# Another clock for the planner that orders a hybrid decoder block: memory told apart by space, durations as measured, eight transfers at once

## The chip, the cores and the metric

The kernel runs on one core of a Trainium2 chip. Its time is the device time of one execution in microseconds (us), here the median of three runs; less is better. The engines named below are PE (TensorE, matrix products, with PEld for its weight loads), DVE (VectorE), ACT (ScalarE), POOL (GpSimd) and SP (SyncE, which issues every DMA). Each engine works through its own instructions strictly in the order in which they were written, so one that waits holds up all that stand behind it on its engine.

## The reference

One decoder block over 2048 tokens of width 1024, all in fp32. An input x is RMS-normed and modulated, and one projection w_in makes 9344 columns of it; two causal token mixers work on them, and three more products bring the result back to the residual stream.

```python
h = _rmsnorm(x, norm_g) * (1.0 + scale) + shift
p = einsum('bsd,de->bse', h, w_in)
c_val, c_gate, c_og, ts, r_og, g_conv, g_rwkv = split(p)
# conv branch: u = val*sigmoid(gate); 31-tap causal depthwise conv; LayerNorm; silu; * silu(c_og); @ w_conv_out
# rwkv branch, per head (16 heads of 64), for every token t:
sk = state @ kk_t
state = state * w_t - sk b_t^T + v_t k_t^T
out_t = state @ r_t
# then a norm over each head, + bonus, * silu(r_og), @ w_rwkv_out
# merge by sigmoid gates g_conv, g_rwkv; @ w_out; residual; final RMSNorm
```

## The kernel before, in words

**Tiling.** Tokens are taken in 4 blocks of 512. w_in has 73 tiles of 128 columns; one projection is 8 slices of the inner dimension by 3 matmuls, since each fp32 operand is split into a high and a low half (h_hi, h_lo; w_hi, w_lo) and high·high, high·low and low·high are summed: 24 "big" matmuls of 128x512 into a PSUM bank called ps_main. In block 0 a weight arrives as w_st, ACT casts its high half w_hi, POOL or DVE subtracts for w_lo, and both halves are stored (kh_in, kl_in) and only loaded again in blocks 1 to 3.

**What runs between the projections.** Per channel tile, the 31 taps of the convolution run on DVE with the sum in PSUM (acc<-u,ck,acc). The recurrence works in chunks of 64 tokens on groups of 4 heads: 16 groups (4 per block, each of two pairs). A group forms masked matrices As, stores a part of them (dA), loads it in another layout (La, with norms dn), inverts triangles on POOL in 31 steps (itmp, TT), stores the result (dT), loads it back into As (As<-dT), transposes on DVE (Tn, Qs) and makes a few products (late, aux, xo are the small PSUM banks; tk, uv and KR are operands of the chain). Then comes its serial chain: 8 steps, each xo<-S,KR on PE, an addition into uv on DVE, xo<-uv,tk on PE, and four updates of the state S on DVE. A group norm follows (gst, POOL, ACT, DVE, grs, POOL: uv<-uv,grs), then two sets of four transposes late<-ident,uv, whose results go as oc through two POOL operations (with zb and zr) to the DRAM tile z_d.

**The output products.** Three products (ro, co, o) for each half of the tokens follow a scheme of seven block products; their weights (w_raw, split into the two halves of w_c) and their operands (cells, h_hi, h_lo) are loaded and split as they are needed. The first product uses two PSUM banks. The others use eight, and wait for that until the last group is normed (`wide[0] = 8` in `lend_cells`, set once the second set of transposes of the last group has been issued).

**What sets the order.** The Python code runs once, when the program is built, and plans with a clock of its own. Every instruction goes through a thin wrapper (`Lane`, so nearly every row of the profile has its line, L186, `r = f(*a, **k)`), which calls `note`. `note` estimates when the instruction starts and ends: `now` is the time of PE, `vt` the time at which each other engine and the DMA become free, `ready` and `used` when a tile is written and read. All side work is a `Task`, a generator that yields a condition: `ok(t)` (t is ready), `idle(engine, us)` (that engine is nearly free), `burst` and `joining` (ready, and some us more), `bank` and `room`. After each big matmul, `poll` lets those tasks go on whose time has come by that clock, and their instructions, small matmuls too, are put there. `until` moves the clock on where PE has nothing to do. `quick` and `some` choose DVE or POOL for a subtraction by which is free earlier, and `Load.steps` chooses so for w_lo. So a wrong estimate does not make a wrong result; it puts an instruction earlier or later in its engine's queue. Waits on the chip are by semaphores.

The estimates before: memory was told apart by the class of a tensor. All tiles from pools have one class, so PSUM tiles and DRAM tiles were both seen as SBUF, and only the kernel's own arguments as DRAM. A transfer takes bytes / 330e3 us on the one DMA time line, and lands 2.8 us later (1.9 if it writes the output). Inputs that are the same object as the output were left out, such as acc in the taps, and the wait between engines was 0.1 us.

Of the kernel before, what the change touches and what calls it, by code (L numbers as in the profile page):

```python
# [15 lines left out]
PSUM = bass.MemoryType.PSUM  # L16
DRAM = bass.MemoryType.DRAM
# [4 lines left out]
TB = 512  # L22
NTT = TB // P
CH = 64
# [38 lines left out]

XN = ((0, 1), (2, 3), (), ())
# [15 lines left out]
def hybrid_block(ctx: ExitStack, tc: tile.TileContext, x, vecs, convk, w2a2, final_g, ada, w_in, w_co, w_ro, w_o, crow, out,  # L80
# [24 lines left out]
    def note(name, op, out, ins, extra=0.0):  # L105
        k_ = key(out)
        t = max([now[0], vt.get(name, 0.0), used.get(k_, 0.0) if name != "PE" or k_[:2] != "xo" else 0.0] + [ready.get(key(a), 0.0) + SEM for a in ins])
        if k_ not in ready and getattr(out.tensor, "tag", None) and out.tensor.name not in cells_:
            past, n = tags.setdefault(out.tensor.tag, []), out.tensor.tag_meta.bufs
            free_ = sorted((max(ready.get(q, 0.0), used.get(q, 0.0)) for q in past), reverse=True)  # L110
            if len(free_) >= n:
                t = max(t, free_[n - 1])
            past.append(k_)
            del past[:-3 * n]
        if name == "PE":
            if op == "transpose":
                part, c = False, 0.11
            else:
                K_, M_, N_ = ins[0].shape[0], size(ins[0]), size(ins[1])
                part = K_ <= 64 or M_ <= 64  # L120
                c = max(N_, 64) / 600 * (0.27 if M_ <= 64 and K_ <= 64 else 0.53 if part else 1.04)
                if ins[1].dtype == F32R:
                    part, c = False, 0.015 + N_ / 2400
            if part != kind[0]:
                kind[0], c = part, c + (0.13 if part else 0.27)
            now[0] = t + c
            end = now[0] + 0.2
        elif name == "SP":
            vt["SP"] = t + 0.47 + (0.2 if k_[:2] in ("dT", "La", "dn") else 0.0)
            vt["DMA"] = max(vt["DMA"], t) + size(out) * out.shape[0] * 4 / DMA_RATE  # L130
            end = vt["DMA"] + (LOAD if on_chip(out) else 2.9 if k_[:2] == "dA" else STORE)
        else:
            n_ = max([size(out)] + [size(a) for a in ins[:1]])
            cols = sum(size(a) == 1 for a in ins[1:])
            wide = [a for a in ins if size(a) > 1]
            if name == "ACT":
                c = (0.065 if in_psum(ins[0]) else 0.105) + 0.82e-3 * n_ + 0.095 * cols + extra
                done_ = 0.1
            elif name == "DVE":
                c, done_ = 0.1 + 1.0e-3 * n_ + 0.05 * min(cols, 1), 0.08  # L140
                if op == "memset":
                    c = 0.1 + 0.9e-3 * n_
                elif n_ <= 16:
                    c = 0.18
                elif op == "scalar_tensor_tensor" and n_ == CH:
                    c = 0.31
                elif op == "tensor_tensor_scan":
                    c += 1.15e-3 * n_
                elif op == "transpose":
                    c += 0.2e-3 * n_  # L150
                elif op == "reciprocal":
                    c = 0.27
                elif in_psum(out):
                    c += 0.13
                elif len(wide) == 1 and not in_psum(ins[0]) and op in ("tensor_scalar", "tensor_copy"):
                    c -= 0.28e-3 * n_
                c += extra
            else:
                c, done_ = (0.1 + 0.72e-3 * n_ if op == "memset" else max(0.2, 0.1 + 2.25e-3 * n_)), 0.045
            both_ = name == "POOL" and op == "tensor_tensor" or name == "DVE" and sum(  # L160
                not in_psum(a) for a in wide) > 1
# [12 lines left out]
        for a in ins:  # L174
            used[key(a)] = max(used.get(key(a), 0.0), end)

    class Lane:
# [4 lines left out]
        def __getattr__(self, op):  # L182
            f = getattr(self.eng, op)

            def call(*a, **k):
                r = f(*a, **k)  # L186
                aps = [x_ for x_ in (*a, *k.values()) if hasattr(x_, "tensor") and hasattr(x_, "shape")]
# [240 lines left out]
    wide = [0]  # L428
# [1238 lines left out]
    with tc.manual_schedule():  # L1667
# [332 lines left out]
        out_ = [e1.tile([P, TB], F32, name=f"mr0_{n}", tag=t_) for n, t_ in  # L2000
                enumerate(("M", "ta", "E2", "k", "r", "vv", "y", "sh", "lw", "la", "E1", "sq"))]
# [210 lines left out]
```

## Time and profile before

| | |
|---|---|
| median of 3 runs | 2774.97 us (2773.39 to 2779.99) |
| profiled execution, its own time | 2775.74 us |
| its span | 2774.0 us |
| PE busy | 2627.9 us (95%) |
| DVE busy | 2225.7 us (80%) |
| POOL busy | 1275.3 us (46%) |
| ACT busy | 1185.1 us (43%) |
| DMA | 705.05 MB, mean 254 GB/s |

The profile is one execution. In a row of groups or of the timeline, "out<-in" are the tiles written and read (numbers left out), "x4" counts instructions, and the bracket gives the idle time of the engine before them and what ended it. A row of waits says which engine waited with which instruction for what, in total, how often and the longest. Matmuls overlap, so the busy time of a row of PE is longer than its share of the time: the mean of one big matmul is 404 ns in the groups, while PE starts one about every 0.23 us.

### The profile page before, as it was taken

To read this page: it belongs to the slowest core of one execution; us is meant where nothing else is said; L and a number is where in the kernel's file an instruction comes from. 1 tells how busy PE (TensorE), PEld (TensorE's weight loads), DVE (VectorE), ACT (ScalarE), POOL (GpSimd) and SP (SyncE) were. 2 spreads that over 40 slices of the span, in tenths; PEclk is the share of its full clock that TensorE was granted. 3 is DMA by queue.
4 is the path that set the end of the run, shared out by engine and by line. 5 is a ranking of instruction groups with operands and counts; after the bars stand their busy time and mean duration, and the time that the engine had idled before them with its cause. 6 is when DMAs were issued, how large, how long until landed. Compare 5 with 4: busy or idle time off the path is not lost. (4 is left out here: it accounts for less than half of the span.)

```text
span 2774.0 us, 51080 instructions
## 1 busy us (share of the span) xinstructions
PE 2627.9 (95%) x18416; PEld 2105.4 (76%) x18416; DVE 2225.7 (80%) x3824; ACT 1185.1 (43%) x2342; POOL 1275.3 (46%) x1791
## 2 busy tenths in 40 slices
PE   6989999999999999999999999999999988999997
PEld 5767777777777777778787878777777776788786
DVE  7777678897878787978788879889887578998586
ACT  5544445453334343434434434323434254546443
POOL 1464756551436654545574737366636557000000
PEclk9999999999999999999999999999999999999999
DMA  8776777866778868877776878777666767889874
GB/s 335 282 258 222 266 265 259 298 220 195 218 231 265 255 217 269 273 262 253 229 255 222 271 249 277 230 269 239 219 227 224 243 223 251 306 305 338 316 256 177
DMA packets 397167, 705.05 MB, mean 254 GB/s; under 512 B 138097, under 2 KB 154801, under 8 KB 396913
## 3 DMA queue, kind: packets, MB, share of 16 engines
q1 hardware_dynamic: 396912, 701.78, 75.2%
q8 instruction: 145, 2.38, 0.3%
q14 instruction: 110, 0.89, 0.1%
HBM read 487.26 MB, written 213.26 MB: 253 GB/s over the span
## 5 line engine op out<-in xcount | busy, mean ns | idle before, releaser
L186 PE MATMUL ps_main<-h_hi,w_lo 128*128 128x512 f32 x2304 | 931.5, 404 | 22.8 <-POOL w_lo L186 17.3
L186 PE MATMUL ps_main<-h_hi,w_hi 128*128 128x512 f32 x2304 | 930.9, 404 | 17.4 <-DMA w_hi<-kh_in 6.9
L186 PE MATMUL ps_main<-h_lo,w_hi 128*128 128x512 f32 x2304 | 927.2, 402 | 0.1
L186 DVE SCALAR_TENSOR_TENSOR acc<-u,ck,acc 128x512 f32<-128x512 f32 x928 | 698.4, 753 | 27.9 <-POOL u L186 0.2
L186 PEld LDWEIGHTS ps_main<-h_hi,w_lo 128*128 128x128 f32 x2304 | 437.8, 190 | 127.0 <-POOL w_lo L186 21.4
L186 PEld LDWEIGHTS ps_main<-h_hi,w_hi 128*128 128x128 f32 x2304 | 438.1, 190 | 118.1 <-issue 15.3
L186 PEld LDWEIGHTS ps_main<-h_lo,w_hi 128*128 128x128 f32 x2304 | 438.2, 190 | 95.3 <-issue 5.3
L186 PE MATMUL ps_main<-h_hi,w_c 128*128 128x512 f32 x896 | 293.7, 406 | 9.4 <-DVE w_c L186 3.2
L186 ACT ACTIVATE th<-ps_main 128x512 f32<-128x512 f32 x160 | 95.7, 598 | 325.2 <-PE ps_main L186 299.4
L186 POOL TENSOR_TENSOR itmp<-La,TT 128x126 f32<-128x126 f32 (+22 forms) x496 | 204.5, 412 | 47.0 <-issue 20.9
L186 POOL TENSOR_TENSOR TT<-TT,itmp 128x126 f32<-128x126 f32 (+22 forms) x496 | 205.3, 414 | 38.9
L186 POOL TENSOR_TENSOR w_lo<-w_st,w_hi 128x1024 fp32r<-128x1024 f32 x56 | 137.9, 2463 | 177.3 <-ACT w_hi L186 160.5
L186 PEld LDWEIGHTS ps_main<-h_hi,w_c 128*128 128x128 f32 x896 | 171.8, 193 | 51.7 <-DVE w_c L186 4.1
L186 DVE SCALAR_TENSOR_TENSOR S<-xo,pe,Se 64x64 f32<-64x64 f32 x512 | 144.9, 283 | 75.8 <-PE xo L186 55.6
L186 PE MATMUL ps_main<-h_lo,w_c 128*128 128x512 f32 x448 | 181.3, 405 | 6.1 <-DVE h_lo L186 5.1
L186 ACT COPY uv<-xo 64x256 f32<-64x256 f32 (+1 forms) x192 | 81.0, 438 | 238.6 <-PE xo L186 173.6
L186 PE MATMUL ps_main<-w_c,h_hi 128*128 128x512 f32 x448 | 140.3, 394 | 0.1
L186 DVE TENSOR_TENSOR As<-aux,maskA 128x512 f32<-128x512 f32 x128 | 82.3, 685 | 55.7 <-PE aux L186 55.0
L186 ACT CAST w_c<-w_raw 128x512 fp32r<-128x512 f32 x168 | 100.6, 617 | 56.1 <-DMA w_raw<-w_co_t 21.4
L186 ACT ACTIVATE t<-ps_main,mu 128x512 f32<-128x512 f32 x96 | 65.8, 685 | 128.6 <-PE ps_main L186 113.5
L186 ACT ACTIVATE Se<-S,pe 128x128 f32<-128x128 f32 x256 | 88.8, 395 | 63.3 <-DVE S L186 62.2
L186 PEld LDWEIGHTS ps_main<-h_lo,w_c 128*128 128x128 f32 x448 | 86.6, 193 | 29.1 <-DVE h_lo L186 8.3
(291 smaller groups left out, 4520.3 us busy)
## 6 DMA issues: line engine op xcount, KB each, us to landing
w_hi<-kh_in SPq DMA_DIRECT2D x219, 512.0 KB
w_lo<-kl_in SPq DMA_DIRECT2D x219, 512.0 KB
w_st<-w_in_t SPq DMA_DIRECT2D x73, 512.0 KB
kh_in<-w_hi SPq DMA_DIRECT2D x71, 512.0 KB
kl_in<-w_lo SPq DMA_DIRECT2D x71, 512.0 KB
lny<-y_d SPq DMA_DIRECT2D x80, 256.0 KB
w_raw<-wk_o SPq DMA_DIRECT2D x56, 256.0 KB
ada_st<-ada_t SPq DMA_DIRECT2D x16, 512.0 KB
```

Of the source, the lines that this page charges most:

```text
L186: r = f(*a, **k)
```

## The change

Only the planner's clock changes; every instruction's work stays as it is.

- `space` reads where a tensor lies from the tensor itself, so PSUM, DRAM and SBUF are told apart.
- Transfers: 405e3 bytes per us in place of 330e3, landing 2.1 us later on chip (2.8 before) and 1.5 us later in DRAM, which now covers DRAM tiles too; five small kinds (dA, dT, La, dn, As) get a fixed time on the line; and a transfer starts no earlier than the landing of the eighth before it (`LANES`).
- The wait between engines is 0.16 us, and the costs of ACT, DVE and POOL are new formulas.
- An engine is free `FREE` earlier than its result is ready (0.085, 0.1 and 0.045 us), so the overlap of successive operations is counted.
- Inputs are picked by the place of the argument, so an in-place operand counts as an input. DVE and POOL are taken to exclude each other only for wide operands in SBUF.

The rows of the diff that matter (`...` is left out):

```diff
-DMA_RATE = 330e3
+DMA_RATE = 405e3
...
-SEM, JOIN, LAG = 0.1, 6.0, 1.0
-LOAD, STORE = 2.8, 1.9
+JOIN, LAG = 6.0, 1.0
+SEM = 0.16
+LOAD, STORE, LANES = 2.1, 1.5, 8
...
+    def space(ap):
+        return str(getattr(ap.tensor, "space", "DRAM")).rsplit(".", 1)[-1]
     def in_psum(ap):
-        return "PSum" in type(ap.tensor).__name__
+        return space(ap) == "PSUM"
     def on_chip(ap):
-        return "DRam" not in type(ap.tensor).__name__
+        return space(ap) != "DRAM"
+    lanes = [0.0] * LANES
+    SLOW = {"dA": 0.2, "dT": 0.79, "La": 1.03, "dn": 0.19, "As": 0.18}
+    FREE = {"DVE": 0.085, "ACT": 0.1, "POOL": 0.045}
...
-            end = now[0] + 0.2
+            end = now[0] + 0.165
         elif name == "SP":
-            vt["SP"] = t + 0.47 + (0.2 if k_[:2] in ("dT", "La", "dn") else 0.0)
-            vt["DMA"] = max(vt["DMA"], t) + size(out) * out.shape[0] * 4 / DMA_RATE
-            end = vt["DMA"] + (LOAD if on_chip(out) else 2.9 if k_[:2] == "dA" else STORE)
+            t = max(t, lanes[0])
+            vt["SP"] = t + 0.45 + (0.2 if k_[:2] in ("dT", "La", "dn") else 0.0)
+            vt["DMA"] = max(vt["DMA"], t) + SLOW.get(k_[:2], size(out) * out.shape[0] * 4 / DMA_RATE)
+            end = vt["DMA"] + (LOAD if on_chip(out) else STORE)
+            lanes.append(end)
+            del lanes[0]
...
-                c, done_ = 0.1 + 1.0e-3 * n_ + 0.05 * min(cols, 1), 0.08
...
-                elif op == "scalar_tensor_tensor" and n_ == CH:
-                    c = 0.31
...
+                fast = len(wide) == 1 and sb and not in_psum(out) and op in ("tensor_scalar", "tensor_copy")
+                c = 0.15 + (0.53e-3 if fast else 2.09e-3 if op == "tensor_tensor_scan" else 1.042e-3) * n_
...
-                c, done_ = (0.1 + 0.72e-3 * n_ if op == "memset" else max(0.2, 0.1 + 2.25e-3 * n_)), 0.045
+                c = 0.1 + 0.72e-3 * n_ if op == "memset" else 0.19 + 0.6e-3 * n_ if op == "tensor_copy" else (
+                    0.17 + (1.7e-3 if n_ == 2 * TB and k_[:2] == "uv" else 2.18e-3) * n_)
...
-            vt[name] = t + c
-            end = vt[name] + done_
+            vt[name] = t + c - FREE[name] + extra
+            end = t + c + extra + (0.035 if name == "POOL" else 0.0)
...
-                note(self.name, op, out_, [x_ for x_ in aps if x_ is not out_ and x_ is not acc_],
-                     0.2 if acc_ is not None else 0.0)
+                ins_ = [x_ for x_ in (*(a if "out" in k else a[1:]), *(v_ for n_, v_ in k.items() if n_ not in ("out", "accum_out")))
+                        if hasattr(x_, "tensor") and hasattr(x_, "shape")]
```

How many instructions there are of each kind stays the same on PE, ACT and SP; on PE there are 9056 big matmuls in both. 18 subtractions and additions move from DVE to POOL (1 for w_lo, 6 for cells, 6 for w_c, 5 for h_lo). Three places show how the order moves.

POOL in block 0, around the first group's norm (uv<-uv,grs is its last multiplication; itmp and TT are the second group's inversion; w_lo is the low half of a streamed weight). Before:

```order
L186 TENSOR_TENSOR vv<-rk,vv 128x512
L186 TENSOR_TENSOR uv<-uv,grs 128x4x256
L186 COPY TT<-dn 64x16 x2
L186 TENSOR_TENSOR itmp<-La,TT 128x31
L186 TENSOR_TENSOR TT<-TT,itmp 128x31
L186 TENSOR_TENSOR w_lo<-w_st,w_hi 128x1024
L186 TENSOR_TENSOR itmp<-La,TT 128x30
```

With the change:

```order
L186 TENSOR_TENSOR itmp<-La,TT 128x2x28
L186 TENSOR_TENSOR TT<-TT,itmp 128x2x28
L186 TENSOR_TENSOR w_lo<-w_st,w_hi 128x1024
L186 TENSOR_TENSOR uv<-uv,grs 128x4x256
L186 TENSOR_TENSOR itmp<-La,TT 128x3x27
L186 TENSOR_TENSOR TT<-TT,itmp 128x3x27
```

The subtraction for w_lo stood behind uv<-uv,grs and the first step of the inversion; it now stands ahead of uv<-uv,grs.

PE in block 2, the first step of a group's chain (S_404 is that group's state). Before:

```order
L186 MATMUL xo<-uv,tk 128x128 x2
L186 MATMUL ps_main<-h_hi,w_lo 128x512
L186 MATMUL ps_main<-h_hi,w_hi 128x512
L186 MATMUL ps_main<-h_lo,w_hi 128x512
L186 MATMUL ps_main<-h_hi,w_lo 128x512
L186 MATMUL ps_main<-h_hi,w_hi 128x512
L186 MATMUL ps_main<-h_lo,w_hi 128x512
L186 MATMUL ps_main<-h_hi,w_lo 128x512
L186 MATMUL ps_main<-h_hi,w_hi 128x512
L186 MATMUL xo<-S_404,KR 128x128 x2
```

With the change:

```order
L186 MATMUL xo<-uv,tk 128x128 x2
L186 MATMUL ps_main<-h_lo,w_hi 128x512
L186 MATMUL ps_main<-h_hi,w_lo 128x512
L186 MATMUL ps_main<-h_hi,w_hi 128x512
L186 MATMUL ps_main<-h_lo,w_hi 128x512
L186 MATMUL ps_main<-h_hi,w_lo 128x512
L186 MATMUL ps_main<-h_hi,w_hi 128x512
L186 MATMUL xo<-S_404,KR 128x128 x2
```

Two big matmuls fewer stand between the step's last product and the next step's first, in which DVE updates S.

PE in the first output product, around the last group's transposes. Before (the second set; the first set, four as well, stands 43 big matmuls ahead of it):

```order
L186 MATMUL ps_main<-h_hi,w_c 128x512 x2
L186 MATMUL ps_main<-h_lo,w_c 128x512
L186 MATMUL ps_main<-h_hi,w_c 128x512
L186 MATMUL late<-ident,uv 128x128 x4
L186 MATMUL ps_main<-h_hi,w_c 128x512
L186 MATMUL ps_main<-h_lo,w_c 128x512
```

With the change:

```order
L186 MATMUL ps_main<-h_hi,w_c 128x512 x2
L186 MATMUL ps_main<-h_lo,w_c 128x512
L186 MATMUL ps_main<-h_hi,w_c 128x512
L186 MATMUL late<-ident,uv 128x128 x8
L186 MATMUL ps_main<-h_hi,w_c 128x512
L186 MATMUL ps_main<-h_lo,w_c 128x512
```

Both sets now stand in one place, where the first product ends, with no big matmul between them.

More of the change, by code (lines that the diff above doesn't have):

```diff
@@ L97, in hybrid_block, with note @@
     port = {"DVE": [], "POOL": []}
+    def space(ap):
+        return str(getattr(ap.tensor, "space", "DRAM")).rsplit(".", 1)[-1]
     def in_psum(ap):
-        return "PSum" in type(ap.tensor).__name__
+        return space(ap) == "PSUM"
     def on_chip(ap):
-        return "DRam" not in type(ap.tensor).__name__
-    def note(name, op, out, ins, extra=0.0):
+        return space(ap) != "DRAM"
+    lanes = [0.0] * LANES
+    SLOW = {"dA": 0.2, "dT": 0.79, "La": 1.03, "dn": 0.19, "As": 0.18}
+    FREE = {"DVE": 0.085, "ACT": 0.1, "POOL": 0.045}
+    def note(name, op, out, ins, extra=0.0, wide=()):
         k_ = key(out)
@@ L134, in note @@
             cols = sum(size(a) == 1 for a in ins[1:])
-            wide = [a for a in ins if size(a) > 1]
+            sb = [a for a in wide if on_chip(a) and not in_psum(a)]
             if name == "ACT":
-                c = (0.065 if in_psum(ins[0]) else 0.105) + 0.82e-3 * n_ + 0.095 * cols + extra
-                done_ = 0.1
+                c = (0.163 if in_psum(ins[0]) else 0.2) + 0.824e-3 * n_ + 0.1 * cols
             elif name == "DVE":
-                c, done_ = 0.1 + 1.0e-3 * n_ + 0.05 * min(cols, 1), 0.08
+                fast = len(wide) == 1 and sb and not in_psum(out) and op in ("tensor_scalar", "tensor_copy")
+                c = 0.15 + (0.53e-3 if fast else 2.09e-3 if op == "tensor_tensor_scan" else 1.042e-3) * n_
                 if op == "memset":
-                    c = 0.1 + 0.9e-3 * n_
-                elif n_ <= 16:
-                    c = 0.18
-                elif op == "scalar_tensor_tensor" and n_ == CH:
-                    c = 0.31
[L147 to L150, printed above, removed]
-                elif op == "reciprocal":
[L152 to L157, printed above, removed]
-            else:
-                c, done_ = (0.1 + 0.72e-3 * n_ if op == "memset" else max(0.2, 0.1 + 2.25e-3 * n_)), 0.045
-            both_ = name == "POOL" and op == "tensor_tensor" or name == "DVE" and sum(
-                not in_psum(a) for a in wide) > 1
+                    c = 0.06 + 0.82e-3 * n_
+                elif op == "reciprocal":
+                    c = 0.35
+                elif n_ > 1:
+                    c += 0.065 * cols
+            else:
+                c = 0.1 + 0.72e-3 * n_ if op == "memset" else 0.19 + 0.6e-3 * n_ if op == "tensor_copy" else (
+                    0.17 + (1.7e-3 if n_ == 2 * TB and k_[:2] == "uv" else 2.18e-3) * n_)
+            both_ = name == "POOL" and op != "memset" or name == "DVE" and (len(sb) > 1 or len(sb) == 1 and fast and n_ > 1)
             if both_:
@@ L186, in call @@
                 r = f(*a, **k)
-                aps = [x_ for x_ in (*a, *k.values()) if hasattr(x_, "tensor") and hasattr(x_, "shape")]
                 out_ = k["out"] if "out" in k else a[0]
                 acc_ = k.get("accum_out")
-                note(self.name, op, out_, [x_ for x_ in aps if x_ is not out_ and x_ is not acc_],
-                     0.2 if acc_ is not None else 0.0)
+                ins_ = [x_ for x_ in (*(a if "out" in k else a[1:]), *(v_ for n_, v_ in k.items() if n_ not in ("out", "accum_out")))
+                        if hasattr(x_, "tensor") and hasattr(x_, "shape")]
+                names = ("in0", "in1", "in_", "data0", "data1")
+                wide_ = [k[n_] for n_ in names if n_ in k] if any(n_ in k for n_ in names) else ins_[:1]
+                note(self.name, op, out_, ins_, 0.12 if acc_ is not None else 0.0, wide_)
                 if acc_ is not None:
```

## The prediction

> **What bounds the kernel now.** First the page's busy times, then windows cut where the work changes: start, block 0, blocks 1 to 3, the seam in which the last groups meet the output products, the products, the tail. A window's columns are us; busy us (and count) of PE, PEld, DVE, ACT, POOL; granted TensorE clock; DMA share; GB/s.
>
> ```profile
> PE 2627.9 (95%) x18416; PEld 2105.4 (76%) x18416; DVE 2225.7 (80%) x3824; ACT 1185.1 (43%) x2342; POOL 1275.3 (46%) x1791
> ...
> 0.00:60.00 60.00, 37.69 (x169) 31.54 (x170) 43.51 (x103) 33.84 (x67) 3.58 (x10) 0.92 0.93 358
> 60.00:780.00 720.00, 676.39 (x4733) 540.19 (x4732) 559.42 (x937) 314.08 (x598) 394.64 (x514) 0.97 0.74 249
> 780.00:2160.00 1380.00, 1344.13 (x10324) 1079.22 (x10323) 1149.43 (x1955) 550.75 (x1128) 763.11 (x1144) 1.00 0.75 247
> 2160.00:2430.00 270.00, 240.61 (x1776) 188.20 (x1775) 211.20 (x354) 121.29 (x233) 114.00 (x125) 0.94 0.75 252
> 2430.00:2759.80 329.80, 329.09 (x1420) 266.26 (x1419) 251.64 (x453) 164.39 (x316) 0.00 (x0) 1.00 0.80 282
> 2759.80:2774.00 14.20, 0.00 (x0) 0.00 (x0) 10.52 (x26) 0.72 (x2) 0.00 (x0) 0.65 0.60 223
> ```
>
> TensorE is the bound. It is idle for 2774.0 − 2627.9 = 146.1 us: 22.3, 43.6, 35.9, 29.4, 0.7 and 14.2 by stage. From 2430 on it only multiplies, one big matmul in 329.8 / 1420 = 0.232 us, the yardstick below. Idle time is not all: a granted clock of 0.97 over 720 us loses 0.03 × 720 = 21.6 us, 0.94 over 270 us loses 16.2. An order can win back at most 43.6 + 35.9 + 29.4 idle and 37.8 of clock. Next, what TensorE waits for (us in total, times, longest):
>
> ```profile
> PE xo L186 <- DVE uv L186: 23.9, 25, 2.3
> ...
> PE ps_main L186 <- POOL w_lo L186: 17.3, 8, 5.9
> ...
> PE late L186 <- DVE Tn L186: 14.6, 20, 1.8
> ...
> PE late L186 <- DVE tk L186: 2.4, 1, 2.4
> ...
> PE ps_main L186 <- DVE w_lo L186: 1.7, 2, 1.3
> ...
> PE late L186 <- DVE Qs L186: 1.5, 1, 1.5
> ...
> PE xo L186 <- DVE S L186: 1.4, 2, 1.0
> ```
>
> These are places where the planner set a matmul ahead of the data it reads; every big matmul behind it in the queue waits too. Those rows are the target.
>
> The change runs nothing on the chip. It alters the planner's clock, so the same work is issued in another order: the terms come from how many big matmuls now stand between a producer and its reader, times 0.232.
>
> **Block 0's streamed weights.** The planner now counts DVE and POOL nearer to what they take, and asks for the low half sooner. The worst waits of before:
>
> ```profile
> 154.26 5.51 DVE L186 SCALAR_TENSOR_TENSOR acc<-u,ck,acc 128x512 f32<-128x512 f32 x7
> ...
> 159.68 0.17 DVE L186 TENSOR_SCALAR dn<-dn 128x32 f32<-128x32 f32 x1
> ...
> 160.36 0.47 POOL L186 COPY TT<-dn 64x16 f32<-64x16 f32 x2 [7.40 <-DVE dn L186]
> ...
> 165.64 0.79 PE L186 MATMUL ps_main<-h_hi,w_lo 128*128 128x512 f32 x1 [5.92 <-POOL w_lo L186]
> ...
> 304.89 1.90 POOL L186 TENSOR_TENSOR uv<-uv,grs 128x1024 f32<-128x1024 f32 x1 [3.50 <-DVE dn L186]
> 306.74 1.48 POOL L186 COPY TT<-dn 64x16 f32<-64x16 f32 x2
> ...
> 308.82 2.35 POOL L186 TENSOR_TENSOR w_lo<-w_st,w_hi 128x1024 fp32r<-128x1024 f32 x1
> ...
> 311.22 0.50 PE L186 MATMUL ps_main<-h_hi,w_lo 128*128 128x512 f32 x1 [3.07 <-POOL w_lo L186]
> ```
>
> Seven taps keep DVE for 5.51 us (0.79 each; the old clock put 0.66, since it dropped the in-place input; the new one puts 0.91). The little operations on dn stand behind them, POOL behind dn, the subtraction behind POOL, TensorE behind that. Of the 68 weights of block 0 that are split as they stream in, those whose cast has under 20 big matmuls ahead of its use fall from 12 to 1 (the subtraction under 10: from 8 to 2). In the second place shown, w_lo now stands ahead of uv<-uv,grs, which spares 1.90 + 1.48 and more. By the subtractions 6/8 of 17.3 + 1.7 = 19.0 goes, 14; by the casts 11/12, 17. I take **−15**; bounds 0 and −19.
>
> What such a wait costs behind itself:
>
> ```profile
> 155.00:159.30 4.30, 4.30 (x20) 3.55 (x19) 4.09 (x7) 1.05 (x1) 0.00 (x0) 1.00 1.04 415
> 159.30:163.00 3.70, 0.42 (x2) 0.00 (x0) 3.63 (x7) 1.95 (x3) 1.14 (x5) 1.00 0.98 353
> 163.10:169.90 6.80, 4.26 (x10) 3.38 (x11) 4.92 (x16) 1.45 (x4) 6.17 (x11) 0.50 0.65 221
> ```
>
> After the stall the clock is 0.50 for 6.8 us. 15 of this stage's 43.6 idle us is a third; a third of its 21.6 us of lost clock gives **−7**, bounds 0 and −21.6. The Trainium skill, in "TensorE: Matmul & The Clock Gate", Part 1 on the HAM clock gate, has the rate fall only after about 3.4 us without work. By it only the 5.92 us wait here pays, with about −3.4 in place of −7, and the whole would come to about 2751; the trace shows 21.6 us lost in the stage, more than its few long waits account for.
>
> **The chain of a group.** Eight steps per group, 128 in all, each: xo<-S,KR; uv on DVE; xo<-uv,tk; four S updates on DVE. Ahead of it come the Tn and tk products.
>
> ```profile
> 1642.21 0.43 DVE L186 TENSOR_TENSOR uv<-xo,uv 64x256 f32<-64x256 f32 x1
> ...
> 1642.69 0.71 PE L186 MATMUL xo<-uv,tk 128*128 128x128 f32 x4 [0.81 <-DVE uv L186]
> ...
> 1643.51 1.22 DVE L186 SCALAR_TENSOR_TENSOR S<-xo,pe,Se 64x64 f32<-64x64 f32 x4 [0.87 <-PE xo L186]
> ...
> 1645.09 0.60 PE L186 MATMUL xo<-S,KR 128*128 128x128 f32 x4
> ```
>
> (a) Ahead of the Tn, Qs and tk products one to two more big matmuls stand (5 to 6 and 9 to 11). Their waits are 14.6 + 1.5 + 2.4 = 18.5 us in 22, 0.84 each; 0.3 more cover takes a third: **−6**, bounds 0 and −18.5. (b) Before xo<-uv,tk stood 4 or 5, now 4 to 7, 0.4 more on average; only 0.1 us a step, but the DVE queue in front of uv no longer holds a tap that the clock thought done: a quarter of 23.9, **−6**, bounds −15 and +5 (the 38 steps that now have 4). (c) The new clock ends the four S updates 0.2 us apart where the row has 0.31, and sets KR 6 big matmuls behind tk where 8 stood, in half of the steps. From the start of the last tk matmul to the end of S the row leaves 1.64 us; six matmuls and the tk itself cover about 1.61. So a small wait at some 60 steps, 0.05 each: **+3**, bounds +1 and +12 (0.2 each). (d) As<-dT is issued 27.4 big matmuls ahead of its first reader, 33.5 before: 1.4 us nearer. DVE has waited there:
>
> ```profile
> DVE Tn L186 <- DMA As<-dT: 15.6, 10, 4.8
> ```
>
> 16 groups by 1.4 is 22, the upper bound; most of it meets waits that (a) covers: **+3**, lower bound 0.
>
> **The seam.** After the last chain the group norm, then two sets of transposes, then the products on eight banks (those wait for the second set).
>
> ```profile
> 2312.31 0.45 PE L186 MATMUL xo<-uv,tk 128*64 128x64 f32 x8 [1.43 <-DVE uv L186]
> ...
> 2315.04 1.22 DVE L186 TENSOR_REDUCE gst<-uv 128x16 f32<-128x1024 f32 x1 [0.49 <-ACT uv L186]
> ...
> 2331.79 1.90 POOL L186 TENSOR_TENSOR uv<-uv,grs 128x1024 f32<-128x1024 f32 x1 [2.26 <-DVE grs L186]
> ...
> 2334.02 0.60 PE L186 MATMUL late<-ident,uv 128*128 128x128 f32 x4
> ...
> 2340.38 1.75 POOL L186 TENSOR_TENSOR oc<-oc,zb 128x512 f32<-128x512 f32 x1
> ...
> 2343.79 1.75 POOL L186 TENSOR_TENSOR oc<-oc,zr 128x512 f32<-128x512 f32 x1
> ```
>
> Before, 43 big matmuls stand between the two sets; now both stand in one place, where the first product ends, 53 big matmuls (12.3 us) behind the last xo<-uv,tk. From that matmul to the first set took 21.7 us (2312.31 to 2334.02), up to 5 of it, by my estimate, behind other work on DVE and POOL: a wait of 4.4 to 9.4, taken as 7. The second set needs the one late bank and two buffers, which the first set's oc work frees. From the first set to the end of oc<-oc,zr it was 11.5 us with other work on POOL between, and the two oc rows and an evacuation alone are some 5; I take 8.5 for the second set. So one wait of 15.5, and 2.5 at half clock: 18. The window lost 29.4 + 16.2 = 45.6 before; half of that stays for its other waits, 23: **−5**, bounds −22 and +10.
>
> **Transfers.** The clock now has a 256 KB load land 2.1 + 0.65 = 2.75 us after its issue, before 2.8 + 0.79 = 3.59. The chain of waits has such loads:
>
> ```profile
> 2413.53 3.80 DMA w_raw<-w_co_t
> ...
> 2418.04 4.88 DMA w_raw<-w_co_t
> ...
> w_raw<-wk_o SPq DMA_DIRECT2D x56, 256.0 KB
> ```
>
> So it is 1.05 to 2.1 us early, where it was 0.2 to 1.3 early. What TensorE reads from transfers has mostly tens of big matmuls of cover; **+5**, bounds 0 and 0.84 × 56 = 47. The Trainium skill, in "DMA: Bandwidth & Descriptors", latency and other measured facts, has HBM latency rise under load, which speaks against one smaller constant; these two rows, 3.80 and 4.88 for one size, agree.
>
> 18 subtractions and additions go from DVE to POOL, at the 1.75 us of the oc rows: **0**, covered by POOL's 54% idle (11 of them now stand 41 instead of 16 big matmuls ahead of their readers); uncovered 31.
>
> **Sum.** −15 − 7 − 6 − 6 + 3 + 3 − 5 + 5 = −28. The profiled execution has span 2774.0, 2775.74 with what lies around it; the median of three, 2774.97, is 0.77 below. Span 2746, so **2747 us**.
>
> **Rivals.** (1) *The gain is given back.* TensorE, free of one wait, runs into the next: DVE is 80% busy in all stages and the chains are serial. Then (a), (b), the clock and the seam give nothing: −15 + 3 + 3 + 5 = −4, **2771**. For it: 25 waits on uv spread over the whole run. Against it: in blocks 1 to 3 TensorE is idle for only 35.9 of 1380 us, so the chains do keep up. (2) *Slower: loads taken as landed too soon.* In the seam and products the low half of w_c, cells and h_lo are set behind a load by the clock's 2.75 us; with 3.80 and more each cast holds ACT, its subtraction DVE or POOL, and a big matmul behind them. If each of the 56 reloads costs the 0.84 by which the allowance shrank, 47 takes the place of my 5: **2789**. It decides once waits on loads cost 33 us. Against it: TensorE waited 0.7 us in 330 us of products, with four loads kept ahead. (3) *A larger gain.* All late weights vanish and the clock stays up: −19 − 16 − 12 − 10 + 4 + 5 − 5 = −53, **2722**. Against it: the single place of the two sets in the seam.
>
> **How the numbers follow.** A difference of 0.3%, 8.3 us, can just be told from none. Chances: forecast 0.55 (its own range 2732 to 2762); given back 0.20, of which a quarter is faster by over 0.3%, 0.6 the same, the rest slower; slower 0.17; larger 0.08. Faster 0.55 + 0.05 + 0.08 = 0.68; same 0.12; slower 0.03 + 0.17 = 0.20. The range takes in the other cases: 2720 to 2788.
>
> **What would show it.** Right: waits on w_lo under 6 us and a clock of 0.98 or more in block 0; uv and Tn waits together under 27 us; one wait of 10 to 20 us before the eight transposes; small waits of KR on S. Wrong: waits on w_hi, w_c, cells or h_lo behind loads above 20 us in all; late<-Tn above 20 us, which would say that As<-dT came too near; a seam that loses over 55 us.

## The result, and the profile after

The changed kernel takes 2804.14 us, the median of 7 runs from 2791.45 to 2814.97; the kernel before, in 7 runs beside it, 2778.96 us (2773.39 to 2783.01). The ratio is 1.0095, with a 95% interval of 1.0072 to 1.0117: slower by 0.95%, where 1% faster was forecast, and outside the range.

The first lines of the page of the changed kernel, and the same windows as before (us; busy us and count of PE, PEld, DVE, ACT, POOL; granted clock; DMA share; GB/s):

```profile
span 2807.0 us, 51073 instructions
...
PE 2646.0 (94%) x18416; PEld 2109.8 (75%) x18416; DVE 2227.3 (79%) x3806; ACT 1189.9 (42%) x2342; POOL 1309.9 (47%) x1809
...
60.00:780.00 720.00, 692.18 (x4867) 553.37 (x4866) 578.47 (x992) 326.60 (x630) 405.46 (x534) 0.99 0.77 258
780.00:2160.00 1380.00, 1323.63 (x10103) 1053.79 (x10102) 1105.73 (x1877) 529.60 (x1078) 749.38 (x1113) 0.99 0.72 237
2160.00:2430.00 270.00, 236.18 (x1755) 183.62 (x1754) 210.28 (x313) 119.24 (x228) 151.43 (x152) 0.94 0.75 248
```

In the first 720 us TensorE now does more (4867 matmuls for 4733) at a clock of 0.99 for 0.97. Then it loses: in blocks 1 to 3 it does 10103 matmuls in the time in which it did 10324, with 1380 − 1323.6 = 56 us idle where 36 were.

Windows of equal time hold unequal work, so the table below goes by work: big matmuls are counted in the trace (a ps_main product of 128x512), and the time is taken from the first to the 2160th (nearly block 0), to the 6720th (blocks 1 to 3), to the 7440th (the seam) and to the end of the products. Idle is time with no matmul running; "long" is what big matmuls took beyond 0.232 us each where one took over 0.35 us; "half clock" is the time for which the trace shows TensorE a granted clock of 0.50.

| | block 0 | blocks 1 to 3 | seam | products |
|---|---|---|---|---|
| before, us | 689.5 | 1419.6 | 242.2 | 351.7 |
| of it idle / long | 39.0 / 21.1 | 40.5 / 26.5 | 26.2 / 14.1 | 3.9 / 3.5 |
| of it at half clock | 35.1 | 17.1 | 23.9 | 6.8 |
| changed, us | 672.3 | 1455.3 | 255.2 | 352.7 |
| of it idle / long | 27.8 / 15.1 | 56.4 / 37.8 | 33.8 / 17.3 | 5.7 / 3.1 |
| of it at half clock | 17.8 | 37.5 | 34.1 | 6.8 |
| difference | −17.2 | +35.7 | +13.0 | +1.0 |

Only a part of the long ones ran at half clock: in blocks 1 to 3, 6.0 of the 26.5 us before and 12.1 of the 37.8 us with the change. The others stand at full clock, next to small products or ahead of a wait.

The waits of TensorE in the changed kernel, and one of DVE (us in total, times, longest):

```profile
PE xo L186 <- DVE uv L186: 21.9, 62, 0.9
PE late L186 <- DVE Tn L186: 20.6, 14, 4.4
...
PE ps_main L186 <- DMA w_hi<-kh_in: 8.9, 1, 8.9
...
PE late L186 <- POOL uv L186: 7.2, 2, 6.9
...
PE ps_main L186 <- POOL w_lo L186: 3.8, 4, 1.5
...
PE xo L186 <- DVE S L186: 0.2, 1, 0.2
...
DVE Tn L186 <- DMA As<-dT: 28.3, 13, 5.6
```

The waits on w_lo are gone as forecast (17.3 to 3.8). The wait on Tn has grown from 14.6 to 20.6, its longest from 1.8 to 4.4, and behind it DVE waits 28.3 us for As<-dT where it waited 15.6. How one of these comes about, from the timeline of the changed kernel (SPq is the queue that issues the transfers; start, us, engine, what, and in brackets the idle time before and what ended it):

```profile
1618.49 4.13 SPq L186 DMA_DIRECT2D As<-dT  x4
1622.71 0.40 SPq L186 DMA_DIRECT2D wk_o<-w_c  x1
1623.23 0.36 SPq L186 DMA_DIRECT2D w_hi<-kh_in  x1
1623.69 0.39 SPq L186 DMA_DIRECT2D w_lo<-kl_in  x1
...
1624.50 0.32 SPq L186 DMA_DIRECT2D wk_o<-w_a  x1
1624.87 1.02 SPq L186 DMA_DIRECT2D As<-dT  x2
...
1629.91 1.23 DVE L186 STREAM_TRANSPOSE Tn<-As 32x256 f32<-32x256 f32 x3 [5.61 <-DMA As<-dT]
1630.86 0.12 PEld L186 LDWEIGHTS late<-Tn,As 32*32 32x32 f32 x1 [4.81 <-DVE Tn L186]
1630.86 0.26 PE L186 MATMUL late<-Tn,As 32*32 32x32 f32 x1 [4.37 <-DVE Tn L186]
```

The last two As<-dT are issued at 1624.87 and 1625.34, behind two loads of 512 KB, and land 5.0 and 4.7 us later; the first of the transposes starts at 1629.91. The planner's clock puts 3.4 us between issue and landing, median over all transfers. The transposes stand in DVE's queue where the clock thought the data was there, so DVE does nothing for 5.61 us (taps and uv stand behind), and TensorE, whose products with Tn stand just as early, waits 4.37 us with every big matmul behind them. In both traces a transfer takes 4.6 us from issue to landing, median over all; the clock of before said 5.3, the new one says 3.4. So the old clock erred on the late side, and the new one errs on the early side.

### The profile page after: what moved, and what is told of

Same layout as the page of the kernel before. It is cut to its first block, busy times and chain, and to the rows that moved or that the text cites. A ratio compares the mean times of both kernels' runs of the same rounds, so it can differ in the third digit from the quotient of the medians.

```text
span 2807.0 us, 51073 instructions
## 1 busy us (share of the span) xinstructions
PE 2646.0 (94%) x18416; PEld 2109.8 (75%) x18416; DVE 2227.3 (79%) x3806; ACT 1189.9 (42%) x2342; POOL 1309.9 (47%) x1809
## 5 line engine op out<-in xcount | busy, mean ns | idle before, releaser
L186 ACT ACTIVATE t<-ps_main,mu 128x512 f32<-128x512 f32 x96 | 65.7, 684 | 108.9 <-PE ps_main L186 100.0
L186 PEld LDWEIGHTS xo<-uv,tk 128*64 128x64 f32 (+1 forms) x768 | 54.0, 154 | 72.5 <-DVE uv L186 70.3
```

## The experiments

Each run compares with the kernel before on the same chip (2773.6 to 2775.7 us, median, in the five sets). A planner's constants move thousands of instructions, so several runs are controls in which a constant moves by so little that an estimate changes by about 0.01 us at most: they show what the accident of one order is worth.

### Which half of the change: transfers or engines

The changed kernel with the transfers' line of before:

```diff
-DMA_RATE = 405e3
-LOAD, STORE, LANES = 2.1, 1.5, 8
+DMA_RATE = 330e3
+LOAD, STORE, LANES = 2.8, 1.9, 8
...
-            t = max(t, lanes[0])
-            vt["SP"] = t + 0.45 + (0.2 if k_[:2] in ("dT", "La", "dn") else 0.0)
-            vt["DMA"] = max(vt["DMA"], t) + SLOW.get(k_[:2], size(out) * out.shape[0] * 4 / DMA_RATE)
-            end = vt["DMA"] + (LOAD if on_chip(out) else STORE)
...
+            vt["SP"] = t + 0.47 + (0.2 if k_[:2] in ("dT", "La", "dn") else 0.0)
+            vt["DMA"] = max(vt["DMA"], t) + size(out) * out.shape[0] * 4 / DMA_RATE
+            end = vt["DMA"] + (LOAD if "DRam" not in type(out.tensor).__name__ else STORE)
```

> The changed kernel with the transfers' line of the clock as it was before (330e3 bytes per us, landing 2.8 us later, no fixed times for dA, dT, La, dn and As, no limit of eight, an issue 0.47 us); engines, spaces and in-place inputs as changed. Theory A, transfers that the clock lets land too soon: most of the 30 us lost is gone; the waits of DVE Tn on As<-dT fall from 28 us to under 18, the last group's transposes stand apart again, 2765 to 2782, ratio 0.997 to 1.002. Theory B, the engines' new costs (taps, S updates, their overlap) thin out the chain: nothing comes back, 2795 to 2810, ratio about 1.008. Theory C, any new order of this kind lands anywhere within 2775 to 2815: no prediction, but then the four runs here show no pattern with the As<-dT lead.

Measured: 2775.15 us, ratio 1.000 (0.9988 to 1.0011). In this order, the only one of its kind, the whole loss is gone; blocks 1 to 3 take 1420.1 us, and the wait of DVE Tn on As<-dT is 10.4 us. But nothing is gained either.

The mirror image, the kernel before with only the changed transfers' line:

```diff
-DMA_RATE = 330e3
-LOAD, STORE = 2.8, 1.9
+DMA_RATE = 405e3
+LOAD, STORE, LANES = 2.1, 1.5, 8
...
+            t = max(t, lanes[0])
...
+            vt["DMA"] = max(vt["DMA"], t) + SLOW.get(k_[:2], size(out) * out.shape[0] * 4 / DMA_RATE)
+            end = vt["DMA"] + (LOAD if not str(getattr(out.tensor, "space", "DRAM")).endswith("DRAM") else STORE)
```

> The kernel before with only the transfers' line of the clock changed (405e3, 2.1 and 1.5 us, the fixed times, eight at once, the real space of the target). Theory A: slower than before although no engine's cost is touched: 2790 to 2810, ratio 1.005 to 1.011, DVE Tn waits on As<-dT above 24 us, one wait of 5 us or more ahead of eight transposes in one place. Theory B: 2770 to 2785, ratio 0.998 to 1.002.

Measured: 2802.2 us, ratio 1.0089 (1.0076 to 1.0102), with no engine's cost touched. Of this run, PE's wait on Tn:

```profile
PE late L192 <- DVE Tn L192: 24.4, 22, 4.9
...
DVE Tn L192 <- DMA As<-dT: 21.9, 10, 7.1
```

Blocks 1 to 3 take 1461.0 us. The second is 21.9, a little under the 24 expected. Its control, 404e3 for 405e3:

> A control of the kernel before with only the changed transfers' line (2802): 404e3 in place of 405e3. If early landings cost as much with the old engine costs as with the new: 2790 to 2812. If they cost little there, and its 2802 was an accident: 2775 to 2788.

Measured: 2793.93 us, 1.0073 (1.0056 to 1.009); blocks 1 to 3 take 1456.3 us. The transfers' line alone makes blocks 1 to 3 slower by over 36 us than in the kernel before; theory B, the engines' new costs as the cause, is out.

### When transfers land

The changed kernel with landings 1.2 us later (in the next two runs the pair is 2.7, 2.1 and 4.5, 3.9, in the third 3.3, 1.5):

```diff
-LOAD, STORE, LANES = 2.1, 1.5, 8
+LOAD, STORE, LANES = 3.3, 2.7, 8
```

> The changed kernel with landings 1.2 us later in the clock (3.3 and 2.7 us), which is what the trace of the changed kernel shows on the mean (4.6 us from issue to landing where the clock has 3.4). Theory A: block 0 keeps its 17 us, blocks 1 to 3 and the seam lose nothing against before: 2755 to 2775, ratio 0.992 to 0.999. Theory B: 2795 to 2810.

Measured: 2767.21 us, ratio 0.9968 (0.9955 to 0.9981): faster than before.

> The changed kernel with landings 0.6 us later (2.7 and 2.1 us), half of what gave 2767. Theory A, the lateness of transfers against the clock sets the loss: between the two, 2778 to 2793, ratio 1.001 to 1.006; DVE Tn waits on As<-dT between 14 and 28 us. If there is a threshold: like one of the two, 2767 or 2803.

Measured: 2777.59 us, 1.0007 (0.9996 to 1.0018), just under the range.

> The changed kernel with landings 2.4 us later (4.5 and 3.9 us), 1.2 us beyond the mean of the trace. Theory A: waits for transfers nearly vanish (DVE Tn on As<-dT under 10 us), but chains and block 0's weights now start later than they could: 2760 to 2780. If caution costs nothing: 2750 to 2762, ratio under 0.996. If it costs as much as haste: above 2785.

Measured: 2768.01 us, 0.9969 (0.9959 to 0.9979). DVE's wait on As<-dT has nearly vanished in it:

```profile
DVE Tn L186 <- DMA As<-dT: 2.0, 2, 1.0
```

From early to late landings the time goes 2804, 2778, 2767, 2768. Beyond the landing that the trace shows (1.2 us more) caution wins nothing in sum: blocks 1 to 3 fall only from 1422.6 to 1418.8 us and the seam from 252.5 to 241.6, while block 0 goes back from 667.6 to 681.8.

Only what lands on chip 1.2 us later:

> The changed kernel with only what lands on chip 1.2 us later (3.3 us), DRAM targets at 1.5. If loads alone carry the loss (a reader stands in an engine's queue ahead of its data): 2762 to 2780. If stores count too (a load issued behind a store that has not landed holds the issuing queue): 2783 to 2797.

Measured: 2762.33 us, 0.9961 (0.9946 to 0.9976). So loads alone carry the loss, as far as one order can tell. (Its wait on As<-dT is still 18.6 us, so that wait alone doesn't set the time.)

Only As<-dT 2 us later:

```diff
-            end = vt["DMA"] + (LOAD if on_chip(out) else STORE)
+            end = vt["DMA"] + (LOAD if on_chip(out) else STORE) + (2.0 if k_[:2] == "As" else 0.0)
```

> The changed kernel with only As<-dT landing 2 us later in the clock, so that 36 big matmuls lie between its last issue and the first product with Tn, as before the change, in place of 27. Theory A with As<-dT as the main transfer: blocks 1 to 3 win back 20 to 30 of their 36 us, the seam stays: 2775 to 2788, ratio 1.000 to 1.003; DVE Tn waits on As<-dT under 12 us. If it is the other transfers (weights, hf, w2a): 2795 to 2805 with those Tn waits gone all the same. Theory B: 2800.

Measured: 2789.15 us, 1.0039 (1.0028 to 1.0051), just above the range expected. Waits of this run:

```profile
PE late L186 <- POOL uv L186: 17.7, 7, 11.3
...
PE late L186 <- DVE Tn L186: 5.2, 9, 1.9
...
DVE Tn L186 <- DMA As<-dT: 8.4, 7, 1.9
```

The waits on Tn fall from 20.6 to 5.2, blocks 1 to 3 from 1455.3 to 1433.2 us, and the seam has a wait of 11.3 us. The time is 15 us under that of the change, and 12 under the mean of its three orders (next section), which is no more than one order is worth; the waits are clear of that (the two controls of the change have 11.2 and 19.3 us on Tn). So As<-dT is a part of the loss, not all of it; no other load was tried alone.

Without the limit of eight:

```diff
-LOAD, STORE, LANES = 2.1, 1.5, 8
+LOAD, STORE, LANES = 2.1, 1.5, 400
```

> The changed kernel without its limit of eight transfers at once in the clock. The last group's two sets of transposes then stand apart again (36 big matmuls), As<-dT has 28 big matmuls ahead of its reader as in the change. Theory A with the landing times as the cause: blocks 1 to 3 stay as slow as in the change, the seam wins back up to 8 us: 2793 to 2806. If the limit of eight is what thinned the order out: 2765 to 2785.

Measured: 2817.67 us, 1.0143 (1.0125 to 1.0161), slower than either theory had it: blocks 1 to 3 take 1466.2 us and DVE waits 31.8 us for As<-dT. The limit doesn't cause the loss. Whether it holds some of it back isn't shown: with it, one of the three orders of the change took 2814 us. The two sets in the seam stand apart again, and the seam takes 247.5 us for 255.2.

### What one order is worth

The changed kernel with 404e3 for 405e3 bytes per us (n1), and with 0.162 for 0.16 us between engines (n2):

> A control: the changed kernel with 404e3 in place of 405e3 bytes per us, which alters no estimate by more than 0.01 us but lets the order fall out a little otherwise. If what a small accident of the order does is small beside the effects read here: 2795 to 2810, ratio 1.006 to 1.012 as for the change. If orders of this kind scatter (theory C), it comes out below 2790 or above 2815.

Measured: 2785.55 us, 1.0036 (1.0023 to 1.0049).

> A second control of the change: 0.162 us in place of 0.16 between engines. With the first at 2786 and the change at 2804: 2780 to 2815. Slower than before by over 0.3% if early landings are the cause; at or below 2775 would say that the loss was an accident of one order.

Measured: 2813.92 us, 1.0143 (1.0122 to 1.0164). Three orders of one clock: 2804, 2786, 2814, mean 2801. The first control falls below 2790: orders of one clock scatter, as theory C has it. The kernel before with 329e3 and with 331e3 for 330e3:

> A control of the kernel before: 329e3 in place of 330e3 bytes per us. Three orders of the change scatter from 2786 to 2814. If before is an ordinary order of its clock: 2768 to 2787. If it was a lucky one (tuned to this order): 2785 or more, and then part of the loss of the change is the end of that luck and not the landing times.

Measured: 2793.92 us, 1.0073 (1.0053 to 1.0094).

> A second control of the kernel before: 331e3 in place of 330e3 bytes per us. The first took 2794 where before takes 2774. If before is a lucky order of its clock: 2780 to 2797. If the first control was an unlucky one: 2768 to 2779.

Measured: 2770.99 us, 0.9988 (0.9976 to 1.000). Three orders of the clock of before: 2775, 2794, 2771, mean 2780. So a single order stands 10 to 15 us to either side of what its clock gives on the mean; of the 29 us between 2775 and 2804 some 21 belong to the change of clock, and the rest can be the accident of the two orders.

By stage the loss is clearer than by the whole. Blocks 1 to 3 take 1419.6, 1421.9 and 1421.3 us in the three orders of before, and 1455.3, 1435.0 and 1443.5 with the change: 24 us more on the mean, and no overlap. The accident sits mostly elsewhere: block 0 takes 689.5, 688.0 and 685.3 us before, 672.3, 684.8 and 683.1 with the change, the seam 242.2, 250.4 and 237.8 before, 255.2, 246.7 and 246.3 with the change.

The runs with later landings have controls too. e3 with 404e3:

> A control of the run with landings 1.2 us later: the same with 404e3 bytes per us, so that the order falls out a little otherwise. If its 2767 was more than luck: 2762 to 2780, below the four orders with landings of 2.1 and 1.5 us. If luck: 2785 and above.

Measured: 2767.37 us, 0.9972 (0.9958 to 0.9985), so 2767 was not luck. The kernel before with the changed transfers' line at 3.3 and 2.7 us, and the same with 404e3:

> The kernel before with the changed transfers' line and landings 1.2 us later (3.3 and 2.7 us), engines' costs, spaces and in-place inputs as before. If the gain of that landing comes from transfers alone: 2760 to 2777, like the one with all costs changed. If the new engine costs add to it: 2775 to 2790. The rule that the waits of DVE Tn on As<-dT go with the time: about 14 us of waits or less at under 2780.

Measured: 2785.78 us, 1.0037 (1.002 to 1.0053).

> A control of the run with the costs of before and landings of 3.3 and 2.7 us (2786): 404e3 in place of 405e3. If the engines' new costs are worth the 19 us by which the run with all costs changed was faster: 2780 to 2795 again. If its 2786 was an accident of one order: 2765 to 2777.

Measured: 2782.06 us, 1.0026 (1.0011 to 1.0041). Put together, in us, each number an order:

| | transfers of before | landing 2.1 / 1.5 | landing 3.3 / 2.7 |
|---|---|---|---|
| engines' costs of before | 2775, 2794, 2771 | 2802, 2794 | 2786, 2782 |
| engines' new costs | 2775 | 2804, 2786, 2814 | 2767, 2767 |

Against landings 1.2 us later, early ones cost 2801 − 2767 = 34 us with the new costs and 2798 − 2784 = 14 with the old ones. Against the transfers of before, the changed line costs 2801 − 2775 = 26 and 2798 − 2780 = 18. The new costs of the engines gain 17 us where landings are late enough, about 5 with the transfers of before (a single order, so within the accident), nothing where landings are early. With the old costs the later landing gives back only a part: blocks 1 to 3 still take 1447.9 and 1440.5 us, 27 and 20 more than the mean before. Why stays open: the waits of those two are many and small, no run takes them apart, and the rate and the fixed times of the five small kinds were not changed alone.

### A version that beats both

Block 0 wants its weights early, the rest its transfers late:

```diff
-LOAD, STORE, LANES = 2.1, 1.5, 8
+LOAD, STORE, LANES = 3.3, 2.7, 8
...
-            end = vt["DMA"] + (LOAD if on_chip(out) else STORE)
+            end = vt["DMA"] + (LOAD if on_chip(out) else STORE) + (1.2 if now[0] > 720 else 0.0)
```

> The changed kernel with landings at 3.3 and 2.7 us up to 720 us of the planner's clock, and at 4.5 and 3.9 us from there on. If block 0 wants weights early (667.6 us up to its 2160th big matmul with 3.3, 681.8 with 4.5) and blocks 1 to 3 and the seam want transfers late (1422.6 and 252.5 us with 3.3, 1418.8 and 241.6 with 4.5): 667.6 + 1418.8 + 241.6 + 348 and the start and tail of about 72 us make a span of 2748, 2745 to 2762 with what an order scatters. If these are accidents of one order: 2765 to 2780.

Measured: 2760.11 us, 0.9946 (0.9929 to 0.9963), with 665.9, 1431.2 and 241.6 us; blocks 1 to 3 took 12 more than in the sum. The control with 404e3:

> A control of the fastest run (landings 3.3 and 2.7 us in block 0, 4.5 and 3.9 us after it, 2760): 404e3 in place of 405e3. If it is more than one lucky order: 2750 to 2772, ratio under 0.998.

Measured: 2755.37 us, 0.9937 (0.9916 to 0.9957), the fastest of all, 667.3, 1420.7 and 244.0 us.

```profile
PE xo L186 <- DVE uv L186: 23.1, 60, 2.4
...
PE ps_main L186 <- DMA w_hi<-kh_in: 11.6, 2, 7.0
...
PE ps_main L186 <- POOL w_lo L186: 3.9, 3, 1.7
```

No wait on Tn is left among its largest, and w_lo stays as low as in the change. What is left is w_hi and uv, the chain's own wait (23.9 before, 21.9 with the change, 23.1 here). Other clocks moved uv, from 14.8 us in the run with only the changed transfers' line to 31.3 with landings 0.6 us later, but not along with the time.

## Why the prediction was wrong

**Two steps failed: what early transfers cost, and what the engines' new costs gain.** The terms put down to the engines, −15 − 7 − 6 − 6 + 3 − 5, come to −36; with the transfers of before those costs brought about 5 us, in one order. The terms on transfers, (d) and the last, come to +8; the changed transfers' line cost 18 us with the old costs and 26 with the new ones. With only the second error the sum would have been +3, with only the first −18 to −10; together they make the loss.

Of the 35.7 us that this order lost in blocks 1 to 3, 15.9 are idle and 11.3 are long big matmuls, of which 6.1 lie in time at half clock; the other 8.5 were not taken apart.

- *Block 0's weights, −15.* Right for the waits: those on w_lo and its like went from 19.0 to 3.8 us. The time follows only in part: −17.2 in this order, −7.5 on the mean of three orders each (687.6 to 680.1), where −22 was reckoned with the clock. The cause given was only partly right too. It was put down to the engines' costs; but the transfers' line alone takes block 0 from 689.5 to 668.1 us, and the engines' costs alone to 679.5. That would follow if a weight that the clock lets land early has its cast issued early, which costs nothing there. "Nearer to what they take" doesn't hold for the taps: at 0.79 us each, the old estimate of 0.66 was 0.13 too short and the new one of 0.91 is 0.12 too long.
- *Half clock there, −7.* Right in this order: time at half clock went from 35.1 to 17.8 us, and what big matmuls lost in it from 13.2 to 5.4, −7.8. The controls have 29.7 and 16.1 us of it with the change, 30.0 and 27.0 before.
- *(a) more cover ahead of Tn and tk, −6.* Half right, and outweighed: waits on tk and Qs are gone (3.9 to nothing), those on Tn grew by 6.0, since the data was late by more than the 0.3 us of cover.
- *(b) uv, −6.* 23.9 to 21.9: −2. Waits became many and short (62 in place of 25, the longest 0.9 in place of 2.3), not fewer us.
- *(c) KR sooner after S, +3.* Wrong and harmless: 1.4 to 0.2.
- *(d) As<-dT nearer its reader, +3, with an upper bound of 22.* This step failed first. It was taken as a wait that (a) covers; but what covers Tn from the side of TensorE doesn't make the transfer land. DVE's wait on As<-dT grew from 15.6 to 28.3 us, TensorE's on Tn by 6.0; the run with As<-dT alone put back is 12 to 15 us faster, within the accident of an order. The prediction's own row, 15.6 us of DVE waiting on As<-dT, showed that this load had no slack, which speaks for a value nearer to its upper bound.
- *The seam, −5.* The one wait came, 6.89 and then 0.87 us where 15.5 were reckoned (16.2 in the second control); the seam still lost 13.0, with 7.2 us of waits on w_c of ACT in that stretch, which were not there before (on h_lo it waits 4.6 us, 5.1 before):

```profile
2383.05 1.11 PE L186 MATMUL late<-ident,uv 128*128 128x128 f32 x4 [6.89 <-POOL uv L186]
2385.04 1.12 PE L186 MATMUL late<-ident,uv 128*128 128x128 f32 x4 [0.87 <-ACT oc L186]
...
2402.43 0.80 PE L186 MATMUL ps_main<-h_hi,w_c 128*128 128x512 f32 x1 [4.06 <-ACT w_c L186]
```

  Without the limit of eight the two sets stand apart, but so they do with it where landings are 1.2 us later (36 big matmuls between them); in the control of that run they stand in one place again. The limit alone isn't what put them together.
- *Transfers landed too early, +5, with an upper bound of 47.* This step was mis-sized most among the terms that were to cost time: 18 to 26 us against the transfers of before, 34 against landings 1.2 us later. The size of the error in the clock was wrong: 0.84 us is what the allowance of one load shrank by when it has the clock's DMA line to itself. That line has a queue in the clock too, and with it the median from issue to landing fell by 1.9 us, from 5.3 to 3.4, past the 4.6 of the traces. And the cover was wrong. "Tens of big matmuls of cover" was read from loads of weights; the loads inside a group's serial path and at a block's start have no such cover, because the planner puts their reader at the very time at which it thinks that they land. As<-dT was shown above; two others of the changed kernel (in all, ACT waits 65.7 us for wf<-w2a in it, 27.7 before):

```profile
784.57 0.40 ACT L186 CAST wl<-wf 128x256 fp32r<-128x256 f32 x1 [8.74 <-DMA wf<-w2a]
...
785.02 0.50 PE L186 MATMUL aux<-lw,wl 128*128 128x512 f32 x1 [2.32 <-ACT wl L186]
...
1699.16 1.94 ACT L186 CAST h_hi<-hf 128x512 fp32r<-128x512 f32 x3 [6.90 <-DMA hf<-xT]
...
1699.83 0.51 PE L186 MATMUL ps_main<-h_hi,w_hi 128*128 128x512 f32 x1 [2.73 <-ACT h_hi L186]
```

  A landing 1.2 us too early isn't a slack used up but a wait at each of them, on two engines that work strictly in order, and then time at half clock.
- *18 operations moved to POOL, 0.* POOL's busy time rose by 34.6 us, and its 47% still covers it; no row looked into shows a cost.

The rival that the loads are taken as landed too soon had the right mechanism for the loss, with a chance of 0.17; its 2789 is 15 us short of this order and 12 short of the mean of three. Its place was wrong: not the reloads in the products, which lost 1.0 us, but the groups of blocks 1 to 3. Of what would have shown the forecast right, two came (waits on w_lo of 3.8 us, a clock of 0.99 in block 0) and two did not (uv and Tn together 42.5 us for 27, a wait of 6.9 us before the eight transposes for 10 to 20); of what would have shown it wrong, "late<-Tn above 20 us" came true. And nothing in the prediction allowed for the accident of an order: 10 to 15 us to either side, as the controls have it, is more than the 8.3 us which was called the line between a change and none.

The rule cited from the Trainium skill, in "DMA: Bandwidth & Descriptors", latency and other measured facts, that HBM latency rises under load, pointed the right way. No run here varies the load, and the rows of 3.80 and 4.88 us show only that one size can differ. What the runs show is the size: 4.6 us from issue to landing at the median where the clock said 3.4.

## What to carry to other kernels

An estimate that sets an order is not judged by its error but by which side it errs on: an operation put a little too late costs a little, one put ahead of its data stops an in-order engine and all that stands behind it, so a landing time belongs at what the trace shows under load or above it, and more so for loads in a serial path. Before a single order is called faster or slower by its clock, move a constant by a hair and time the orders that come out: here they lie up to 23 and 28 us apart, and it is the times by stage that tell a loss from an accident. And a load that DVE or TensorE already waits for has no slack, so a microsecond by which it comes nearer to its reader is better counted near its full price.

## What the runs showed of the hardware that was not expected

The clock falls after shorter waits than expected. In the kernel before, a wait of 1.59 us that ends at 1492.24 was followed by 4 us at 0.66, and in the changed kernel the wait of 4.37 us by 3 us at 0.50 and 4 us at 0.58:

```profile
1490.00:1493.00 3.00, 1.41 (x51) 0.95 (x51) 1.65 (x4) 0.11 (x1) 0.58 (x2) 1.00 1.01 402
1493.00:1497.00 4.00, 4.00 (x38) 3.19 (x33) 3.74 (x8) 0.00 (x0) 1.02 (x1) 0.66 0.40 150
...
1631.00:1634.00 3.00, 3.00 (x67) 2.74 (x66) 2.94 (x5) 0.62 (x1) 1.66 (x2) 0.50 0.89 339
1634.00:1638.00 4.00, 4.00 (x22) 2.87 (x23) 1.98 (x5) 0.00 (x0) 1.72 (x2) 0.58 0.10 36
```

In "TensorE: Matmul & The Clock Gate", Part 1, the Trainium skill asks for about 3.4 us without work; the measurement decides. Up to the end of the products the half clock comes in these two traces in stretches of 3.41, 6.83 or 10.24 us, and in the 3.41 us ahead of a stretch TensorE was idle for 1.3 to 3.4 us. Not each such wait pays: of 26 waits of 1.4 us or more in the kernel before, from 98 us on, 18 were followed by half clock within 3.5 us of their end. A stretch of 3.41 us at half clock costs 1.7 us of work, about as much as the wait. So the −7 that was reckoned from the lost clock was nearer (−7.8 in this order) than the −3.4 by that rule.

Behind one small store the next transfers landed late. In the changed kernel's timeline one issue stands 8.93 us:

```profile
698.67 0.43 SPq L186 DMA_DIRECT2D grow_d<-hgate_col  x1
...
701.15 0.37 SPq L186 DMA_DIRECT2D w_hi<-kh_in  x1
701.63 0.37 SPq L186 DMA_DIRECT2D w_lo<-kl_in  x1
702.09 8.93 SPq L186 DMA_DIRECT2D gr_d<-th  x1
711.12 0.69 SPq L186 DMA_DIRECT2D y_d<-yj  x1
```

The store grow_d<-hgate_col, 4 KB in elements of 4 bytes, is issued at 698.67 and lands 10 us later, and w_hi<-kh_in, issued behind it at 701.15, 14.3 us later, for which TensorE waits the 8.9 us of the list above. From 702 to 711 us the core moves 37 to 81 GB/s, where its mean is 251. In the kernel before it is the same: the store takes 10.9 us, the w_hi behind it 14.1, and TensorE waits 4.6 us. (In the table by work the wait of 8.9 falls in block 0, that of 4.6 in blocks 1 to 3.) That this store is what held the others was not tried by a run.

The limit of eight, which the new clock copies, is the program's and not the chip's. The program gives its transfers eight semaphores in turn, and an issue waits until the transfer before it on its semaphore has landed: over the whole run no issue comes ahead of that landing, and 299 of 2347 come within 0.3 us behind it. It isn't what held gr_d<-th for 8.93 us, since the eighth before it had landed at 700.8; what did stays open.
